# A hybrid attention block: three weight halvings moved to VectorE, two loads asked for earlier, one halving held back

## The chip, the cores and the metric

The kernel runs on one core of a Trainium2 chip. The time is that of the device for one execution, in microseconds (us). A core has five engines that run side by side and wait for each other through semaphores: TensorE (PE) multiplies matrices, VectorE (DVE), ScalarE (ACT) and GpSimd (POOL) work element by element, and SyncE (SP) only asks for transfers (DMA). Each engine takes its instructions in the order in which they stand in its queue. All DMAs of this kernel are asked for by SP, so they too have one order.

## What is computed

One decoder layer over 512 positions and 16 leading learned positions, width 1024: a projection, two attention branches with 16 heads each, a gated sum, and an output projection.

```python
u = rmsnorm(h, pre_norm_g)
cq, ckv, k_pe_raw, z_mla, fq, fk, fv, f_logit, z_fox, gate_a, gate_b = split(u @ w_in)
o_mla = causal_attention(q_m, k_m, v_mla, MLA_SCALE)          # q, k, v from cq, ckv, k_pe_raw
y_mla = (o_mla * silu(z_mla)) @ w_br_mla
cum = cumsum(log_sigmoid(f_logit + fox_forget_b))
o_fox = causal_attention(fq, fk, fv, FOX_SCALE, cum)          # logit[t,s] += cum[t] - cum[s]
y_fox = (o_fox * silu(z_fox)) @ w_br_fox
mixed = (sigmoid(gate_a) * y_mla + sigmoid(gate_b) * y_fox) @ w_out
h = h + rmsnorm(mixed, post_norm_g)
```

## The kernel before

**Precision.** Products are made from two 16-bit or 32-bit halves of each number: a high half (a rounded copy) and a low half (what the copy lost), in three matmuls: high by high, high by low, low by high. So each unit of weights, 128 columns of `w_in` (128 x 1024 numbers, 512 KB), is first loaded (`wraw`), then *halved*. For the class `Halved` this goes in steps: a bound of the numbers is found (`peak`, by ScalarE into `junk` or by VectorE's reduction at line 203), a small matmul into the `scale` bank with lines 216 to 219 makes it a power of two (`sc`), ScalarE writes the high half (line 258), and the low half follows in `lower`: on GpSimd in two instructions (lines 271 and 272, the first of which overwrites `wraw`), or on VectorE in one (line 269). Which of them it is stands in `low[0]`. While the list `deferred` is not empty, the low half isn't issued but put on that list, to be issued later. `held` names an instruction behind which a low half must stand.

**Stages.** After an opening that normalizes the input and makes the small projections, 16 stages run, one for each pair of heads and each branch, in turn FoX (`br` 1) and MLA (`br` 0): `stages`, numbered `si`. A stage has, in TensorE's order, the scores of its own pair (`st`, into six PSUM banks: two of `acc`, `b0`, `b1`, `c0`, `c1`), then the product with the values of the *stage before* (`ov`), and then a `fill`: the projections that later stages need. A FoX stage fills with the gates' projections `z` (`za`, `zb`) of this pair and `mq`, `mk`, `v` of the next MLA stage; an MLA stage fills with `fq`, `fk`, `v` of the next FoX stage. In the first stage the `fill` also has the first output gate, `pg`.

Scores go from PSUM to SBUF by VectorE (`evict`, line 979: `sf`, with the row bound `nb`), ScalarE takes exponentials (line 1014), VectorE inverts the sums (lines 1018 and 1019: `su`, `ri`), and the normalized probabilities become two 16-bit halves in `pn`: the 16 leading columns by GpSimd (`mt`, lines 1034 to 1039), the rest by ScalarE (high, line 1049) and VectorE (low, line 1053). Four DMA transposes per stage write them to `pt` (line 98); a further one writes the values' halves `vh` (lines 903 to 912, from the banks `c0` and `c1`) to `vp`. `ov` needs both, and its result is taken up by VectorE at line 1089 (`gT`). In the first stage `pt` also serves as room for the rotary product of MLA's queries, whose halves GpSimd writes to `gT` (lines 854 and 110) when `pg` has read the last of the input's 32-bit copies, whose room `gT` takes; they go through DRAM (`qpe_dram`) to `QP`.

**Order.** TensorE's instructions stand as the program issues them. On the other engines a scheduler orders them by priority: what is issued under `tc.high_priority` goes ahead, `tc.issue_after(x)` puts an instruction behind `x`. Loads stand in SP's queue where `w.load()` is called, once the transfers there are kept in program order.

**Weights ahead.** `sets[si]` are the units whose peaks are found and whose halving begins in stage `si`: for the first stage (`si` 0) the q, k and v of the third stage (`si` 2); for the second stage the two z of the second pair, which the third stage's `fill` uses. The first three loads of `sets[0]` are asked for in the opening; the two of `sets[1]` and three of `sets[2]` in the first stage, behind its four `pt` transposes. The first two units of `sets[0]` are halved at the end of the first stage's `fill` (the last two entries), the third in the second stage (`middles`). `first_z` are the two gates' weights z of the first pair. The low half of the first of them (`w_865` below) is put off and issued by VectorE at the end of the opening. Raw weights rotate through a few rooms; the fifth load counted from `sets[0]` takes the room that held the first of `first_z`.

Of the kernel before, what the change touches and what calls it, by code (L numbers as in the profile page):

```python
# [17 lines left out]
ALU = mybir.AluOpType  # L18
# [38 lines left out]
def block_kernel(ctx: ExitStack, tc: tile.TileContext, x, meta_tokens, pre_norm_g, w_in, fox_forget_b,  # L57
# [665 lines left out]
    with ExitStack() as att:  # L723
# [146 lines left out]
        def v_unit(br, pr):  # L870


            st = {}
            if br == 0:
                get = lambda: by_k(mw[pr][3], 1)
                nk, act = 1, ckv_act
            else:
                nk = KD
                get, act = (win_w(O_FV, pr), u_act) if pr else (early, both_act)

            def done(i, ps):
                if i == 0:
                    st["sc"] = aw.tile([128, 16], F32, tag="vsc", name=f"vsc{br}{pr}", bufs=4)
                    st["ps"] = ps
                sc = st["sc"]
                nc.vector.tensor_reduce(out=sc[:, i : i + 1], in_=ps, op=ALU.max, axis=AX.X, apply_absolute_value=True)
                if i == 0:
                    return
                nc.vector.tensor_scalar(out=sc[:, 2:3], in0=sc[:, 0:1], scalar1=sc[:, 1:2], scalar2=None, op0=ALU.max)
                nc.vector.tensor_single_scalar(out=sc[:, 2:3].bitcast(I32), in_=sc[:, 2:3].bitcast(I32),  # L890
                                               scalar=0x7F800000, op=ALU.bitwise_and)
                nc.vector.tensor_scalar(out=sc[:, 2:3], in0=sc[:, 2:3], scalar1=2.0 ** -100, scalar2=2.0 ** -14,
                                        op0=ALU.max, op1=ALU.mult)
                nc.vector.reciprocal(sc[:, 3:4], sc[:, 2:3])

                if br and pr:
                    nc.gpsimd.tensor_scalar(out=sc[:, 4:5], in0=sc[:, 2:3], scalar1=get.r, scalar2=2.0 / PSCALE, op0=ALU.mult,
                                            op1=ALU.mult)
                else:
                    nc.gpsimd.tensor_scalar(out=sc[:, 4:5], in0=sc[:, 2:3], scalar1=1.0 / PSCALE, scalar2=None, op0=ALU.mult)  # L900

                lead = st["ps"][:, 0:META]
                nc.scalar.activation(vh[:, 0, 0:64].rearrange("p (r c) -> p r c", c=32)[:, :, 0:META],
                                     lead.unsqueeze(1).broadcast_to([128, 2, META]), AF.Copy, scale=sc[:, 3:4])
                parts = [(vh[:, 0, 64 : 64 + META], lead, vh[:, 0, 0:META])]
                for q, p in enumerate((st["ps"][:, META:], ps)):
                    p = p.rearrange("p (j c) -> p j c", c=128)
                    hi, lo = (vh[:, 4 * q + 1 : 4 * q + 5].rearrange("p (j l) c -> p j l c", l=2)[:, :, l] for l in range(2))
                    nc.scalar.activation(hi, p, AF.Copy, scale=sc[:, 3:4])  # L909
                    parts.append((lo, p, hi))  # L910
                for lo, p, hi in parts:
                    nc.vector.scalar_tensor_tensor(out=lo, in0=p, scalar=sc[:, 3:4], in1=hi, op0=ALU.mult, op1=ALU.subtract)  # L912
                vsc[br, pr] = sc

            def tr():
                dma(vps[br], vh.rearrange("p t c -> p (t c)"), nc.sync.dma_start_transpose)
            return unit(f"v{br}{pr}", get, act, nk, ALLT, done, two("c")), [(0, tr)]
# [247 lines left out]
        def by_vector(w):  # L1165
            low[0] = nc.vector
            w()
            low[0] = nc.gpsimd

        def loads_of(ws):  # L1170
            return call(*[w.load for w in ws])
        fills, middles = [], []
        for si, (br, pr) in enumerate(stages):
            last = si + 1 == len(stages)
            ws = sets[si]
            if br == 1:
                za, zb = zs[pr]
                q, k, v = feeds[si + 1]
                fill = (vts[br, pr] if pr else begun) + za + q + zb[:3] + k + zb[3:5] + v + (call(ws[0]) if si else []) + zb[5:] + (call(ws[0]) if not si else []) + call(lambda ws=ws, p=stages[si + 1]: after_keys(ws[1], p[1]))
                middles.append([])  # L1180
            else:
                q, k, v = last_gates if last else feeds[si + 1]
                if last:
                    fill = vts[br, pr] + q + k + call(ws[0].scale, *[lambda w=w: by_vector(w) for w in ws]) + v
                else:
                    fill = vts[br, pr] + q + k[:KD] + v[:4] + call(ws[0].scale, ws[0]) + v[4:8] + call(lambda n=si + 1: peaks(sets[n][2:], nc.vector)) + v[8:] + call(ws[1]) + k[KD:]
                middles.append([sets[si - 1][2]])
            if br and si:
                fill += sum(map(loads_of, sets[si + 2 : si + 3]), [])
            if si == 5:  # L1190
                pe, rest1, store1, _ = pe_unit(1)
                fill[24:24] = pe
            fills.append(fill)
# [34 lines left out]
        deferred[:] = [None]  # L1228
        first_z[0]()
        run(opening[len(pe0) + KD : -4])  # L1230
        low[0] = nc.vector
        deferred.pop()()
        deferred.clear()
        low[0] = nc.gpsimd
        cycle[0] = 7
        loads[0] = 0
        for w in sets[0]:
            w.load()
        run(opening[-4:])
        behind.clear()  # L1240
# [1 line left out]
        for si, (br, pr) in enumerate(stages):  # L1242
# [7 lines left out]
            if si == 0:  # L1250

                run(begun)
                gT += [const.tile([128, KD, S], F32, tag=f"tokenuT{n}", name=f"gT{i}") for i, n in enumerate("hl")]
                run(fill[4:5])
                run(vts[1, 0] + pe_rest)
                between.append(lambda: load_qp(0))
                n0()
                low[0] = nc.vector
                for ahead_ in [fn.prep for _, fn in fill[5:] if hasattr(fn, "prep")][:2]:
                    first[:] = [60]  # L1260
                    with tc.issue_after(whole[0]):
                        ahead_()
                    first.clear()
                low[0] = nc.gpsimd
                n1()
                with tc.issue_after(turned_p[0]):
                    bias(1)
                peaks(sets[0], nc.scalar)
                run(fill[5:9])
                for w in sets[1] + sets[2]:  # L1270
                    w.load()
                run(fill[9:])
            else:
                run(fill[:3])
                if si == 3:
                    with tc.issue_after(turned_p[0]):
                        stores(4, 8)
                run(fill[3:5])
                if si == 1:

                    behind[:] = exps[:1]
                if si == 2:
                    behind.clear()
                n0()
                if pr and not (br or last):
                    bias(pr + 1)
                if br:
                    sets[si][0].scale()
                for job in middles[si]:
                    job()  # L1290
                if not br and si > 1:
                    run(loads_of(sets[si]))
                run(fill[5:9])
                run(fill[9:11])
                if si == 5:
                    pe[0][1].prep()
                if br:

                    behind[:] = [halved[("k", 1, pr), 1]]
                run(fill[11:12])  # L1300
                if br:
                    behind.clear()
                n1()
                if not br:
                    if last:
                        peaks(sets[si][:1], nc.scalar)
                        peaks(sets[si][1:], nc.vector)
                    else:
                        peaks(sets[si], nc.scalar)
                        peaks(sets[si + 1][:1], nc.vector)  # L1310
                        with tc.issue_after(lowered[("q", 1, pr + 1), 0]):
                            peaks(sets[si + 1][1:2], nc.vector)
                if not (br or last):
                    masked_bias()
                if 6 <= si < 8:

                    written[0] = True
                    rest1(si - 6)
                    written[0] = False
                if 8 <= si < 10:  # L1320
                    written[0] = True
                    with tc.issue_after(turned_p[0]):
                        store1(si - 8, 2, 8)
                    written[0] = False
                run(fill[12:])
# [376 lines left out]
```

## Time and profile before

| | us |
|---|---|
| median of 3 runs | 587.65 (587.45 to 588.69) |
| profiled execution | 587.34 |
| its span, first to last instruction | 585.6 |
| TensorE busy | 565.6 |
| VectorE busy | 469.1 |
| ScalarE busy | 391.0 |
| GpSimd busy | 242.9 |

The rows of the profile's views have the engine, the line of the kernel, the operation, the tile written and the tiles read (`out<-in`), the shape, and how many equal instructions are counted together (`x`). In a timeline the first two numbers are start and length in us from the start of the span, and in brackets stands how long the engine was idle before and who ended that. Line 104 is every matmul, line 98 every transfer kept in order. Busy shares are averages over stages with different limits; a gap on TensorE has to be found in its own stage.

### The profile page before, as it was taken

To read this page: it belongs to the slowest core of one execution; us is meant where nothing else is said; L and a number is where in the kernel's file an instruction comes from. 1 tells how busy PE (TensorE), PEld (TensorE's weight loads), DVE (VectorE), ACT (ScalarE), POOL (GpSimd) and SP (SyncE) were. 2 spreads that over 40 slices of the span, in tenths; PEclk is the share of its full clock that TensorE was granted. 3 is DMA by queue.
4 is the path that set the end of the run, shared out by engine and by line. 5 is a ranking of instruction groups with operands and counts; after the bars stand their busy time and mean duration, and the time that the engine had idled before them with its cause. 6 is when DMAs were issued, how large, how long until landed. Compare 5 with 4: busy or idle time off the path is not lost.

```text
span 585.6 us, 11322 instructions
## 1 busy us (share of the span) xinstructions
PE 565.6 (97%) x3864; PEld 401.6 (69%) x3864; DVE 469.1 (80%) x1248; ACT 391.0 (67%) x859; POOL 242.9 (41%) x352
## 2 busy tenths in 40 slices
PE   8999989799999999999999999999999999999995
PEld 6988556556766667658567676644776775688884
DVE  6868789669788889887797888779958987468966
ACT  7867796678787777876876878874443463343762
POOL 4422757565685697774756846800000000000000
PEclk9999998899999999999999999999999999999998
DMA  8515699969999789899998895857933230333603
GB/s 294 112 53 154 173 176 309 236 138 236 170 212 249 159 183 170 187 209 179 223 248 184 162 222 128 183 109 234 307 106 108 73 109 1 107 109 108 216 0 144
DMA packets 220026, 97.74 MB, mean 167 GB/s; under 512 B 131353, under 2 KB 209569, under 8 KB 219969
## 3 DMA queue, kind: packets, MB, share of 16 engines
q1 hardware_dynamic: 219968, 97.03, 69.5%
q8 instruction: 30, 0.49, 0.3%
q14 instruction: 28, 0.22, 0.1%
HBM read 62.62 MB, written 4.23 MB: 114 GB/s over the span
## 4 chain that ended last, share of the span: by engine, by line
PE 83%; DVE 7%; DMA 4%; issue 2%; ACT 2%; POOL 2%; SPq 0%; DVEq 0%; POOLq 0%
PE z L104 17%; PE pg L104 10%; PE v L104 7%; PE py L104 7%; PE fk L104 7%; PE fq L104 7%; PE x L104 6%; PE st L104 6%; PE ov L104 6%; DMA pt<-pn 3%; PE psm L104 2%; PE mq L104 2%; PE y L104 2%; DVE w L269 1%; PE mk L104 1%
## 5 line engine op out<-in xcount | busy, mean ns | idle before, releaser
L104 PEld LDWEIGHTS <-w 128*128 128x128 f16 x1584 | 150.1, 98 | 114.5 <-issue 4.3
L1014 ACT ACTIVATE sf<-sf,nb 128x272 f32<-128x272 f32 (+3 forms) x128 | 72.6, 569 | 21.5 <-DVE nb L979 19.2
L272 POOL TENSOR_TENSOR w<-wraw,w 128x1024 f16<-128x1024 f32 x38 | 81.5, 2144 | 2.5
L104 PE MATMUL z<-hTh,w 128*128 128x512 f16 x256 | 82.4, 382 | 0.0
L1053 DVE SCALAR_TENSOR_TENSOR pn<-sf,ri,pn 128x512 f16<-128x512 f32 (+3 forms) x128 | 74.1, 637 | 2.1 <-ACT pn L1049 2.1
L104 PE MATMUL pg<-hTh,w 128*128 128x512 f16 x240 | 72.6, 379 | 0.8 <-DVE w L269 0.8
L219 POOL TENSOR_SCALAR sc<-sc,su 128x2 f32<-128x2 f32 (+2 forms) x22 | 8.3, 378 | 142.6 <-DVE sc L216 142.4
L258 ACT ACTIVATE w<-wraw,sc 128x1024 f16<-128x1024 f32 x43 | 48.3, 1144 | 24.2 <-DVE sc L218 18.4
L1049 ACT ACTIVATE pn<-sf,ri 128x128 f16<-128x128 f32 (+3 forms) x128 | 59.7, 547 | 5.2 <-issue 3.8
L271 POOL TENSOR_SCALAR wraw<-wraw,sc 128x1024 f32<-128x1024 f32 x38 | 43.3, 1140 | 23.6 <-ACT w L258 22.4
L104 PE MATMUL z<-hTl,w 128*128 128x512 f16 x128 | 48.8, 381 | 0.0
L110 DVE TENSOR_TENSOR wl<-wraw,w 128x512 fp32r<-128x512 f32 (+1 forms) x44 | 38.5, 881 | 11.9 <-PE scale L104 4.1
L104 PE MATMUL pg<-hTl,w 128*128 128x512 f16 x120 | 45.5, 379 | 0.0
L104 PE MATMUL ov<-pt,vp 128*64 128x512 f16 (+4 forms) x416 | 35.8, 327 | 8.1 <-DMA pt<-pn 6.0
L104 PE MATMUL st<-hlk,hlq 64*128 64x272 f32 (+4 forms) x480 | 42.2, 299 | 1.1 <-DVE vh L912 1.1
L104 PE MATMUL fk<-hTh,w 128*128 128x272 f16 (+1 forms) x224 | 40.1, 276 | 0.0
L104 PE MATMUL v<-hTh,w 128*128 128x272 f16 (+1 forms) x224 | 39.3, 276 | 0.0
L104 PEld LDWEIGHTS <-vp 128*64 128x64 f16 (+1 forms) x416 | 23.9, 116 | 22.1 <-issue 13.0
L104 PEld LDWEIGHTS st<-hlk,hlq 64*128 64x128 f32 x480 | 33.5, 186 | 6.6 <-ACT vh L909 2.8
L104 PE MATMUL fq<-hTh,w 128*128 128x512 f16 x112 | 34.7, 381 | 0.0
L1405 ACT CAST w<-wraw 128x512 fp32r<-128x512 f32 x28 | 16.7, 616 | 23.5 <-DVE wraw L1414 19.0
L165 ACT CAST w<-wraw 128x1024 fp32r<-128x1024 f32 (+1 forms) x20 | 20.2, 1014 | 17.0 <-PE py L104 15.3
(342 smaller groups left out, 1476.7 us busy)
## 6 DMA issues: line engine op xcount, KB each, us to landing
wraw<-in_w_in_dram SPq DMA_DIRECT2D x47, 512.0 KB
room<-in_w_in_dram SPq DMA_DIRECT2D x9, 512.0 KB
cbp<-c_dram SPq DMA_DIRECT2D x16, 264.0 KB
wraw<-in_w_br_fox_dram SPq DMA_DIRECT2D x8, 512.0 KB
tb<-in_w_out_dram SPq DMA_DIRECT2D x8, 512.0 KB
wraw<-in_w_br_mla_dram SPq DMA_DIRECT2D x8, 512.0 KB
wraw<-in_w_out_dram SPq DMA_DIRECT2D x6, 512.0 KB
QP<-qpe_dram SPq DMA_DIRECT2D x8, 256.0 KB
```

What stands on the lines that cost most here:

```text
L104: nc.tensor.matmul(*a, **k)
L110: return eng.tensor_tensor(out=lo, in0=src, in1=f32(hi), op=ALU.subtract)
L165: nc.scalar.copy(wh[:, :n], raw[:, :n])
L219: nc.gpsimd.tensor_scalar(out=r, in0=t, scalar1=su[:, 5:6], scalar2=1.0, op0=ALU.mult, op1=ALU.mult)
L258: self.hi = nc.scalar.activation(hi, raw, AF.Copy, scale=self.s).ins
L269: nc.vector.scalar_tensor_tensor(out=lo, in0=raw, scalar=self.s, in1=hi, op0=ALU.mult, op1=ALU.subtract)
L271: nc.gpsimd.tensor_scalar(out=raw, in0=raw, scalar1=self.s, scalar2=1.0, op0=ALU.mult, op1=ALU.mult)
L272: nc.gpsimd.tensor_tensor(out=lo, in0=raw, in1=hi, op=ALU.subtract)
L1014: exps[b // 3] = nc.scalar.activation(sf, sf, AF.Exp, bias=sums["nb"][:, h, b : b + 1], scale=-1.0, accum_out=sums["su"][:, h, b : b + 1]).ins
L1049: normed[:] = [nc.scalar.activation(hi, sf, AF.Copy, scale=rib).ins]
L1053: nc.vector.scalar_tensor_tensor(out=lo, in0=sf, scalar=rib, in1=hi, op0=ALU.mult, op1=ALU.subtract)
L1405: nc.scalar.copy(to[0], src)
```

## The change

Four things are done. The low half of the first of `first_z` is now held behind the last instruction that writes `vh` in the opening (`lowered["v"]`). The loads of `sets[1]` are asked for in the opening, behind those of `sets[0]`, and only those of `sets[2]` in the first stage. The low halves of `sets[0]` (the third stage's q, k and v) are made by VectorE instead of GpSimd: the first two are put off from the first stage's end to the second stage, where they are issued right behind the scores, the third is made in the second stage as before but by VectorE. Last, in the second stage the scale and the first halving of the next z units stand behind four more steps of `v`.

```diff
@@ v_unit, done @@
                 for lo, p, hi in parts:
-                    nc.vector.scalar_tensor_tensor(out=lo, in0=p, scalar=sc[:, 3:4], in1=hi, op0=ALU.mult, op1=ALU.subtract)
+                    lowered["v"] = nc.vector.scalar_tensor_tensor(out=lo, in0=p, scalar=sc[:, 3:4], in1=hi, op0=ALU.mult, op1=ALU.subtract).ins
@@
+        def lower_by_vector():
+            low[0] = nc.vector
+            for fn in deferred[1:]:
+                fn()
+            deferred.clear()
+            low[0] = nc.gpsimd
+
@@ fills of the MLA stages @@
-                    fill = vts[br, pr] + q + k[:KD] + v[:4] + call(ws[0].scale, ws[0]) + v[4:8] + call(lambda n=si + 1: peaks(sets[n][2:], nc.vector)) + v[8:] + call(ws[1]) + k[KD:]
+                    fill = vts[br, pr] + q + k[:KD] + v[:4] + (call(ws[0].scale, ws[0]) + v[4:8] if pr else v[4:8] + call(ws[0].scale, ws[0])) + call(lambda n=si + 1: peaks(sets[n][2:], nc.vector)) + v[8:] + call(ws[1]) + k[KD:]
@@ opening @@
         run(opening[len(pe0) + KD : -4])
-        low[0] = nc.vector
-        deferred.pop()()
-        deferred.clear()
-        low[0] = nc.gpsimd
+        held[:] = [lowered["v"]]
+        lower_by_vector()
+        held.clear()
         cycle[0] = 7
         loads[0] = 0
-        for w in sets[0]:
+        for w in sets[0] + sets[1]:
             w.load()
@@ first stage @@
-                for w in sets[1] + sets[2]:
+                for w in sets[2]:
                     w.load()
-                run(fill[9:])
+                run(fill[9:-2])
+                deferred[:] = [None]
+                run(fill[-2:])
             else:
+                if si == 1:
+                    lower_by_vector()
                 run(fill[:3])
...
                 for job in middles[si]:
-                    job()
+                    by_vector(job) if si == 1 else job()
```

The instructions of TensorE are the same but for the place of one `scale` matmul; ScalarE's are the same. On the other queues the change shows at these places.

VectorE at the end of the opening, before (`v_827` and `v_867` are the two halves of the first FoX values, `vsc` their scale, `w_865` the first gate's weights):

```order
L886 TENSOR_REDUCE vsc_852<-v_827 128x1
L269 SCALAR_TENSOR_TENSOR w_865<-wraw_817,sc_819,w_865 128x1024
L886 TENSOR_REDUCE vsc_852<-v_867 128x1
L889 TENSOR_SCALAR vsc_852<-vsc_852 128x1
L890 TENSOR_SCALAR vsc_852<-vsc_852 128x1
```

And VectorE there now, down to the first score eviction:

```order
L886 TENSOR_REDUCE vsc_852<-v_827 128x1
L886 TENSOR_REDUCE vsc_852<-v_867 128x1
L889 TENSOR_SCALAR vsc_852<-vsc_852 128x1
L890 TENSOR_SCALAR vsc_852<-vsc_852 128x1
L892 TENSOR_SCALAR vsc_852<-vsc_852 128x1
L894 RECIPROCAL vsc_852<-vsc_852 128x1
L912 SCALAR_TENSOR_TENSOR vh<-v_827,vsc_852,vh 128x16
L912 SCALAR_TENSOR_TENSOR vh<-v_827,vsc_852,vh 128x2x128
L912 SCALAR_TENSOR_TENSOR vh<-v_867,vsc_852,vh 128x2x128
L269 SCALAR_TENSOR_TENSOR w_865<-wraw_817,sc_819,w_865 128x1024
L979 ISA sf_931,nb_928<-st_933,cbp_745 128x144
```

The gate's halving went from between the two reductions to between the last `vh` and the first eviction.

VectorE at the start of the second stage now (`w_1181` and `w_1183` are the third stage's q and k weights; before, line 979 followed line 912 there without a halving between them):

```order
L912 SCALAR_TENSOR_TENSOR vh<-v_1147,vsc_1145,vh 128x2x128
L269 SCALAR_TENSOR_TENSOR w_1181<-wraw_905,sc_1067,w_1181 128x1024
L269 SCALAR_TENSOR_TENSOR w_1183<-wraw_907,sc_1067,w_1183 128x1024
L979 ISA sf_1188,nb_1185<-st_1190,maskt 128x272
L979 ISA nb_1185 128x1
```

Though issued behind the scores, the two halvings stand ahead of all of that stage's evictions; the third stands ahead of its `pn`.

SP from the second stage's bias loads (`cbp`) to its first `pt` transpose, before (`wraw_1079` and `wraw_1081` are `sets[1]`, the next three `sets[2]`):

```order
L1103 DMA cbp_746<-c_dram 128x528
L98 DMA wraw_1079<-in_w_in_dram 128x8x128
L98 DMA wraw_1081<-in_w_in_dram 128x8x128
L98 DMA wraw_1083<-in_w_in_dram 128x8x128
L98 DMA wraw_1085<-in_w_in_dram 128x8x128
L98 DMA wraw_1087<-in_w_in_dram 128x8x128
L98 DMA_TRANSPOSE vp_760<-vh 128x9x128
L98 DMA wraw_1604<-in_w_uq_dram 128x2x192
L98 DMA wraw_1604<-in_w_ukv_dram 128x256
L98 DMA wraw_1763<-in_w_in_dram 128x8x128
L98 DMA QP<-qpe_dram 128x512
L98 DMA wraw_1765<-in_w_in_dram 128x8x128
```

And SP at the same place now:

```order
L1103 DMA cbp_746<-c_dram 128x528
L98 DMA wraw_1083<-in_w_in_dram 128x8x128
L98 DMA wraw_1085<-in_w_in_dram 128x8x128
L98 DMA_TRANSPOSE vp_760<-vh 128x9x128
L98 DMA wraw_1087<-in_w_in_dram 128x8x128
L98 DMA wraw_1601<-in_w_uq_dram 128x2x192
L98 DMA wraw_1601<-in_w_ukv_dram 128x256
L98 DMA wraw_1760<-in_w_in_dram 128x8x128
L98 DMA QP<-qpe_dram 128x512
L98 DMA wraw_1762<-in_w_in_dram 128x8x128
L98 DMA_TRANSPOSE pt<-pn_756 128x6x128
```

Two of the seven 512 KB loads that stood ahead of the second stage's `pt` transposes are gone from there (they stand ahead of the first stage's `vp` now, behind the first three), and `vp` went ahead of one.

## The prediction

> **What bounds the kernel now.** I read the page first.
>
> ```profile
> PE 565.6 (97%) x3864; PEld 401.6 (69%) x3864; DVE 469.1 (80%) x1248; ACT 391.0 (67%) x859; POOL 242.9 (41%) x352
> PEclk9999998899999999999999999999999999999998
> wraw<-in_w_in_dram SPq DMA_DIRECT2D x47, 512.0 KB
> ```
>
> TensorE is busy for 97% of the span, so the time can fall only where TensorE stands still or runs at a lower clock. Each digit of the clock row is 14.6 us; the two eights, 88 to 117 us, are the only dip before the end. Next, whom TensorE waits for, in the view of waits:
>
> ```profile
> PE ov L104 <- DMA pt<-pn: 6.0, 3, 4.0
> PE st L104 <- DVE vh L912: 1.1, 1, 1.1
> ```
>
> Then where these stand, in the chain of work between 55 and 135 us (start, length, what):
>
> ```profile
> 63.31 0.61 DVE vh L912 x2
> ...
> 64.06 1.11 PE st L104 x6
> ...
> 85.11 1.95 issue
> 87.05 3.46 PE ov L104 x26
> ...
> 106.66 6.19 DMA pt<-pn
> ...
> 112.99 3.84 PE ov L104 x26
> ```
>
> There are three gaps, all in the first three stages: 1.1 us before 64.06 (the first stage's third set of scores waits for VectorE to empty the value banks), 1.95 before 87.05 (the second stage runs the first stage's `ov`; its transposed probabilities `pt` land only then), and 3.97 before 112.99 (the same, one stage later). A fourth loss is the clock, in the windows (last columns: granted clock, DMA share, GB/s):
>
> ```profile
> 86.00:90.00 4.00, 2.95 (x22) 2.17 (x24) 2.31 (x9) 4.00 (x12) 3.92 (x3) 0.68 0.84 251
> 90.00:94.00 4.00, 4.00 (x24) 1.89 (x21) 3.83 (x7) 3.34 (x9) 3.93 (x10) 0.89 1.15 345
> 110.00:114.00 4.00, 1.01 (x6) 0.61 (x8) 2.90 (x21) 3.91 (x14) 2.12 (x5) 0.67 1.07 249
> 114.00:118.00 4.00, 4.00 (x27) 2.25 (x23) 1.08 (x4) 0.23 (x1) 0.16 (x1) 0.50 1.10 282
> 118.00:122.00 4.00, 4.00 (x20) 1.83 (x19) 3.14 (x9) 4.00 (x9) 2.72 (x9) 0.98 0.12 30
> ```
>
> After the gaps of 1.95 and 3.97 the clock is halved for a while; after the gap of 1.1 it is not (the clock row shows nines there).
>
> **The change, part by part.** *First gate held.* VectorE halves the first gate's weights between the two reductions of `v`; now it does so behind the last `vh`.
>
> ```profile
> 59.36 1.94 DVE L269 SCALAR_TENSOR_TENSOR w<-wraw,sc,w 128x1024 f16<-128x1024 f32 x1 [0.94 <-ACT w L258]
> 63.30 1.02 DVE L912 SCALAR_TENSOR_TENSOR vh<-v,vsc,vh 128x16 f16<-128x16 f32 x3 [0.83 <-POOL cbm L1112]
> 67.99 1.17 POOL L854 CAST gT<-pt 128x512 fp32r<-128x512 f32 x2 [3.41 <-PE pg L104]
> 74.08 4.09 SPq L98 DMA_TRANSPOSE pt<-pn  x2
> ```
>
> `vh` ends 1.94 earlier, more than the 1.1 TensorE waits, so the gap goes. Queued behind the held instruction are the score evictions; they do not get later, since as much went from in front of them. The gate's own matmuls come behind `pg`, which ends at 67.99: over 3 us to spare. Whether the end gains depends on the next gap: TensorE must not merely arrive 1.1 earlier at the same `pt`. GpSimd's casts at 67.99 wait for `pg` on TensorE and so move with it, and the transposes at 74.08 follow that GpSimd chain. So `ov` at 87.05 moves by nearly as much, and the gap of 1.95 stays. Bounds: 0 (all swallowed at 87) and 1.1. I take **1.05**, near the gap's own row, as all links follow TensorE.
>
> *Two loads a stage sooner, and the third stage's weights off GpSimd.* Both work on the 3.97:
>
> ```profile
> 58.44 4.05 SPq L98 DMA_DIRECT2D wraw<-in_w_in_dram  x3
> 85.50 7.53 SPq L98 DMA_DIRECT2D wraw<-in_w_in_dram  x5
> 99.09 10.87 SPq L98 DMA_TRANSPOSE pt<-pn  x4
> 120.44 7.85 SPq L98 DMA_TRANSPOSE pt<-pn  x4
> 84.93 2.13 POOL L272 TENSOR_TENSOR w<-wraw,w 128x1024 f16<-128x1024 f32 x1
> 98.14 0.80 POOL L1038 TENSOR_TENSOR pn<-mt,pn 128x96 f16<-128x96 f32 x1
> 106.76 2.26 PE L104 MATMUL st<-hlk,hlq 64*128 64x272 f32 x30
> ```
>
> The four transposes are asked for from 99.09 to 109.96 and have landed at 112.85 (106.66 + 6.19). Two things hold them: the SP queue, which is full from 85.5 on with five loads in front, and GpSimd's last part of `pn`, done at 98.94. Two of the five loads go: 512 KB at 345 GB/s is 1.52 each, **3.04** together. GpSimd loses three halvings (the row at 84.93 is the longer half of one), so its part is no longer last. With the 1.05 from before, `pt` lands at 112.85 - 3.04 - 1.05 = 108.76, while TensorE, now done with the scores at 106.76 + 2.26 = 109.02, arrives at 107.97: a rest of 0.8. But the four transposes took 7.85 to ask for in the next stage, with a queue less full, against 10.87 here: up to 3.0 more, and no rest. I take a rest of 0.3, so **3.67** of the 3.97. Bounds: 0 (they move only as TensorE does) and 3.97.
>
> The two loads now stand in front of the first stage's `vp` and `pt` transposes. They cost the same 3.04 there, asked for from 62.5. The three loads before them and they need 5 x 1.52 = 7.6 from 58.44, with about one load's worth of bias loads ahead, and so end near 68; the transposes are wanted from 73. That idle queue is the cover; without it the first stage's `pt` comes up to 3.04 late. The second of them also takes the room of the first gate's raw weights, and so waits for the held halving, with `vp` behind it in SP's queue; that halving is over by 64.3 as all of VectorE's work there, and `vp` is read at 87. I take 0.
>
> *Clock.* `ov` takes 3.84 after the gap; at full clock:
>
> ```profile
> 134.37 2.04 PE L104 MATMUL ov<-pt,vp 80*64 80x512 f16 x26
> ```
>
> That is 1.8 more, and z runs at half clock for another 1.4 us, losing 0.7: **2.5** that go with the gap, if the rest is short. Bounds 0 and 2.5. The half clock after 87.05 stays with its gap.
>
> *VectorE.* It takes on three halvings, two in front of the second stage's score evictions, one in front of its `pn`:
>
> ```profile
> L269 DVE SCALAR_TENSOR_TENSOR w<-room,sc,w x9: 1276/1278/1289, 419.9 to 494.4; 128x1024 f16<-128x1024 f32 x9
> 89.16 1.24 DVE L1018 SCALAR_TENSOR_TENSOR su<-su 128x6 f32<-128x6 f32 x1 [0.78 <-ACT sf L1014]
> 91.32 7.40 DVE L1053 SCALAR_TENSOR_TENSOR pn<-sf,ri,pn 128x512 f16<-128x512 f32 x8
> 138.79 4.40 DVE L1053 SCALAR_TENSOR_TENSOR pn<-sf,ri,pn 128x512 f16<-128x512 f32 x8
> 106.21 1.02 DVE L912 SCALAR_TENSOR_TENSOR vh<-v,vsc,vh 128x16 f16<-128x16 f32 x3 [0.72 <-ACT vh L909]
> ```
>
> 3 x 1.28 = 3.84 (5.82 at the 1.94 of the row at 59.36). Against that, the eight `pn` took 7.40 beside GpSimd's halvings and take 4.40 two stages later, and the small `su` took 1.24, a microsecond too much, beside one of them: 3.0 + 1.0 back. Even, so `vh` at 106.21 stays and no score waits for it. I take 0. Without that cover it is the slow rival below.
>
> *Scale moved* behind four more steps of v:
>
> ```profile
> 100.01 0.17 PE L104 MATMUL scale<-sc,spread 128*128 128x2 bf16 x1
> 101.96 0.14 DVE L216 TENSOR_SCALAR sc<-scale 128x2 int32<-128x2 int32 x1
> ```
>
> Its result lies 1.9 us unread; twelve matmuls of 0.12 are 1.4. Nothing.
>
> *What is late next.* With 7 us gone, stage three's own transposes (120.44) must follow:
>
> ```profile
> 113.29 0.61 ACT L1014 ACTIVATE sf<-sf,nb 128x400 f32<-128x400 f32 x1
> ```
>
> Its exponentials end at 113.9 whatever TensorE does; today the rest waits for `ov`. So the transposes can come 4 earlier, issued by 128.29 - 4 = 124.3, and landing some 2.9 later (as 109.96 to 112.85), at 127.2; TensorE reaches 134.37 - 7.2 = 127.2. No margin: I charge **0.2**.
>
> *Sum.* 1.05 + 3.67 + 2.5 - 0.2 = 7.0. The profiled execution took 587.34 (span 585.6), the median is 587.65: 587.34 - 7.0 = 580.3, and 0.3 for the median: **580.6**. Later gaps of `ov` (2.0 together, in the row of 6.0) move rigidly with TensorE, as their transposes wait for what TensorE produces.
>
> **Rivals.** *Partial.* The transposes get only half of the 3.97, 2.0 remain and with them the half clock, as after the gap of 1.95: 1.05 + 2.0 = 3.0 off, 584.6. For it: the DMA share is over 1 in those windows, so fewer loads may just let others fill the queue. Against: the loads removed are a large part of it. The windows show 0.68 right after a gap of 1.95, so I price a gap of 2 with the half clock. The Trainium skill, TensorE: Matmul & The Clock Gate, What's actually happening, states that the clock falls after at least one idle window of about 3.4 us. By that rule a rest of 2.0 keeps the full clock and this rival gives 584.6 - 2.5 = 582.1; the trace does not agree with it at 87.
>
> *More.* The 1.95 shrinks too, if the first stage's transposes gain more than TensorE does: up to 1.95, and 3.46 - 2.04 = 1.4 of clock: 577.2. Little speaks for it, since the GpSimd chain follows TensorE.
>
> *Nothing.* The first gap is swallowed at 87 and the second stays, because the transposes, not the loads, fill the queue: 587.6. Against: GpSimd's 98.94 and five loads stand plainly in front of 99.09.
>
> *Slower.* VectorE becomes the bound in the second stage: each halving takes 1.94, nothing comes back, and `vh` at 107.23 ends 5.8 later, at 113.0. The next scores wait for it as those at 64.06 did, `ov` starts at 114.1 instead of 112.99 with the half clock kept: 588.8. It decides from 4.7 late on. Against: the halvings leave GpSimd, and the 1.94 was measured beside GpSimd's work of 58.9 to 62.6. The Trainium skill, SBUF — State Buffer, SBUF: two separate sides, states that a VectorE instruction with two SBUF inputs and a GpSimd instruction that reads SBUF lock each other out whole. By that rule each halving can lose one of the GpSimd instructions that remain, 0.80 as at 98.14: 3 x 2.08 = 6.2 in place of 5.8, and 589.2; that the eight `pn` took 7.40 against 4.40 agrees with a lock.
>
> **How the numbers follow.** Forecast 0.58 (own range 579.0 to 582.5), partial 0.17, more 0.08, nothing 0.09, slower 0.08. The range reaches from the fast rival to the partial one, 577.0 to 585.0, and leaves out 0.17. A measurement of this kernel tells about 0.2% from no change: faster 0.83, same 0.09, slower 0.08.
>
> **What would show it.** First step: no wait of `st` for `vh`, and `ov` near 86.0. Second: five loads in the SP queue near 58 and two near 84.5, `pt` transposes asked for by 96, `ov` of the third stage near 108 with under 1 us of waiting. Clock: 1.00 from 94 on. VectorE: eight `pn` in under 5 us although a halving stands ahead. Wrong would be a first-stage `pt` that is no earlier (1.95 grows to 3), a wait of `st` for `vh` near 107, or a new wait of `ov` near 127.

## The result, and the profile after

| | before | after |
|---|---|---|
| median, us | 587.65 | 580.46 (580.19 to 582.48) |
| profiled execution, us | 587.34 | 580.54 |
| its span, us | 585.6 | 578.8 |
| mean granted clock | 0.989 | 0.995 |

The ratio of the times is 0.988, with a 95% interval from 0.985 to 0.991: the changed kernel is 7.2 us faster, against 7.0 forecast. A fourth run of the kernel before took 640.87 us, far above the others, and is left out as a slow one. The clock row of the changed kernel has one eight where two stood side by side:

```profile
PE 563.0 (97%) x3864; PEld 399.8 (69%) x3864; DVE 468.0 (81%) x1251; ACT 390.8 (68%) x859; POOL 232.1 (40%) x346
PEclk9999998999999999999999999999999999999999
```

Whom TensorE waits for, in the view of waits (total, times, longest):

```profile
PE ov L104 <- DMA pt<-pn: 4.7, 4, 2.4
PE scale L104 <- DVE hlk L110: 0.6, 1, 0.6
```

The wait of `st` for `vh` is gone, and the longest wait of `ov` is now that of the first stage. The second row is new, and the prediction did not name it: at 80.05 TensorE waits for VectorE's `hlk`. Every profile with the gate held has this wait of 0.6 to 0.7 in the `scale` matmul, and none without has it. Then SP's queue in the timeline (start, length, what):

```profile
56.92 0.80 SPq L1103 DMA_DIRECT2D cbp<-c_dram  x2
58.17 7.03 SPq L98 DMA_DIRECT2D wraw<-in_w_in_dram  x5
...
72.34 4.32 SPq L98 DMA_TRANSPOSE pt<-pn  x2
...
77.61 5.96 SPq L98 DMA_TRANSPOSE pt<-pn  x2
...
85.07 1.04 SPq L98 DMA_DIRECT2D wraw<-in_w_in_dram  x2
...
94.20 11.42 SPq L98 DMA_TRANSPOSE pt<-pn  x4
```

Five loads stand near 58 and two near 85, as the change says. The third stage's four transposes, the row at 94.20, are asked for earlier than at 99.09, and take 11.42 to ask for where they took 10.87. And the chain of work through the first three stages:

```profile
80.21 6.31 DMA pt<-pn
86.66 2.66 PE ov L104 x26
...
108.62 1.97 PE ov L104 x26
110.59 2.70 PE z L104 x12
113.29 2.61 PE z L104 x12
...
127.50 1.97 PE ov L104 x26
```

No transfer stands ahead of the third stage's `ov` at 108.62 any more, and it runs at full clock. To compare executions, times are counted below from SP's ask for the first bias loads, the row `cbp` at 56.92 here. In the kernel before that row is:

```profile
57.19 0.81 SPq L1103 DMA_DIRECT2D cbp<-c_dram  x2
```

The steps of its chain that were not shown ahead are:

```profile
116.83 3.39 PE z L104 x12
...
120.22 2.61 PE z L104 x12
...
134.44 1.97 PE ov L104 x26
```

So counted, the first stage's `ov` went from 29.86 to 29.74, the third stage's from 55.80 to 51.70, and the second group of z behind it (120.22 before, 113.29 now) from 63.03 to 56.37. The gain is therefore 0.12 up to the first `ov`, 3.98 more up to the third, and 2.56 in that `ov` (3.84 to 1.97) and the z behind it (3.39 to 2.70). From there everything moves along: the fourth stage's `ov` starts 6.67 earlier, the span is 6.8 shorter.

### The profile page after: what moved, and what is told of

It is laid out like the page before. It is cut to its first block, busy times and chain, and to the rows that moved or that the text cites. A ratio compares the mean times of both kernels' runs of the same rounds, so it can differ in the third digit from the quotient of the medians.

```text
span 578.8 us, 11317 instructions
## 1 busy us (share of the span) xinstructions
PE 563.0 (97%) x3864; PEld 399.8 (69%) x3864; DVE 468.0 (81%) x1251; ACT 390.8 (68%) x859; POOL 232.1 (40%) x346
## 4 chain that ended last, share of the span: by engine, by line
PE 77%; DVE 8%; DMA 5%; ACT 4%; issue 2%; POOL 2%; SPq 1%; DVEq 0%; ACTq 0%; POOLq 0%
PE z L104 15%; PE pg L104 10%; PE py L104 8%; PE fq L104 7%; PE v L104 7%; PE x L104 6%; PE fk L104 6%; PE st L104 5%; PE ov L104 5%; DMA pt<-pn 4%; PE psm L104 2%; PE mq L104 2%; PE y L104 2%; DVE w L269 1%; DVE wl L110 1%
## 5 line engine op out<-in xcount | busy, mean ns | idle before, releaser
L272 POOL TENSOR_TENSOR w<-wraw,w 128x1024 f16<-128x1024 f32 x35 | 74.9, 2141 | 2.3
L1053 DVE SCALAR_TENSOR_TENSOR pn<-sf,ri,pn 128x512 f16<-128x512 f32 (+3 forms) x128 | 70.9, 611 | 1.6 <-ACT pn L1049 1.6
L271 POOL TENSOR_SCALAR wraw<-wraw,sc 128x1024 f32<-128x1024 f32 x35 | 39.8, 1136 | 20.5 <-ACT w L258 19.4
L104 PE MATMUL ov<-pt,vp 128*64 128x512 f16 (+4 forms) x416 | 33.2, 311 | 4.7 <-DMA pt<-pn 4.7
L104 PEld LDWEIGHTS <-vp 128*64 128x64 f16 (+1 forms) x416 | 22.3, 111 | 17.7 <-issue 6.9
```

The costliest lines, as they stand in the source:

```text
L104: nc.tensor.matmul(*a, **k)
L271: nc.gpsimd.tensor_scalar(out=raw, in0=raw, scalar1=self.s, scalar2=1.0, op0=ALU.mult, op1=ALU.mult)
L272: nc.gpsimd.tensor_tensor(out=lo, in0=raw, in1=hi, op=ALU.subtract)
L1053: nc.vector.scalar_tensor_tensor(out=lo, in0=sf, scalar=rib, in1=hi, op0=ALU.mult, op1=ALU.subtract)
```

## The experiments

Three groups of four kernels ran, each group on one chip beside its own runs of the kernel before, so totals are given as ratios to that, with their 95% intervals. The times of the kernel before spread over 4.5 to 7.5 us within a group, so the reading goes by the profiles, one for each kernel: when an `ov` starts after the ask for the bias loads, and how long TensorE stood idle before it. The changed kernel was not run on the first group's chip; that group's totals can only be set beside its ratios on two others, 0.988 and 0.986.

### One part of the change undone

**The gate.** The halving goes back between the two reductions:

```diff
-        held[:] = [lowered["v"]]
-        lower_by_vector()
-        held.clear()
+        low[0] = nc.vector
+        deferred.pop()()
+        deferred.clear()
+        low[0] = nc.gpsimd
```

> The changed kernel with the first gate's halving back between the two reductions of v. Theory S (swallowed: the first stage's transposes land at their own time, near 86.5, whatever TensorE does before): the wait of st for vh of 1.1 us is back at 64, the gap before the first stage's ov shrinks from 2.4 to between 1.3 and 1.9, that ov starts at 86.6 +- 0.3, total as the changed kernel, 580.5 +- 0.5. Theory P (the prediction's own step): ov starts 1.05 later, at 87.7, total 581.5. Rival R: the halving that runs earlier frees its room earlier for the fifth load, so the first stage's vp and pt come earlier, ov at 86.2 or less, total 579.5 to 580.3.

Ratio 0.992 (0.989 to 0.995). From the timeline (in brackets how long TensorE was idle, and who ended it):

```profile
57.64 0.80 SPq L1103 DMA_DIRECT2D cbp<-c_dram  x2
...
64.52 1.11 PE L104 MATMUL st<-hlk,hlq 64*128 64x400 f32 x6 [1.20 <-DVE vh L912]
...
87.90 3.44 PE L104 MATMUL ov<-pt,vp 80*64 80x512 f16 x26 [1.93 <-DMA pt<-pn]
```

The wait for `vh` is back, and `ov` starts 30.26 after the ask, 0.52 later than the 29.74 of the changed kernel. That lies between S (no change) and P (1.05 later); R falls. The total, 3.5 us under the kernel before, is worse than P's 581.5, but its interval overlaps that of the changed kernel.

**The loads.** Both go back behind the first stage's transposes:

```diff
-        for w in sets[0] + sets[1]:
+        for w in sets[0]:
...
-                for w in sets[2]:
+                for w in sets[1] + sets[2]:
```

> The changed kernel with the two loads of sets[1] back in the second stage's queue. Theory Q (additive: the loads carry 3.04 of the 3.97, GpSimd's part the rest): the third stage's ov has a gap of about 3.0 again and the half clock with it, total 580.5 + 3.0 + 2.5 = 586.0. Theory B (both ends in one: the transposes wait for whichever of queue and GpSimd is later): gap 3.5 to 4, total 586.5 to 587.3. Rival G (GpSimd's part alone carried it): gap under 1, total 581 or less. For the first stage, theory L (the two early loads slow its transposes): ov of the first stage starts 0.5 to 1.0 earlier than the changed kernel's 86.66, at 85.7 to 86.2; theory S (they have a landing time of their own): no change.

Ratio 0.999 (0.997 to 1.001): without the loads the rest of the change is worth nothing that can be measured. From the timeline:

```profile
57.48 0.80 SPq L1103 DMA_DIRECT2D cbp<-c_dram  x2
...
86.14 2.04 PE L104 MATMUL ov<-pt,vp 80*64 80x512 f16 x26 [1.79 <-issue]
...
111.34 3.84 PE L104 MATMUL ov<-pt,vp 80*64 80x512 f16 x26 [4.45 <-DMA pt<-pn]
```

The gap before the third stage's `ov` is whole again, 4.45, so G falls, Q's 3.0 is too little, and B's 3.5 to 4 is the nearest. The first `ov` starts at 28.66, 1.08 earlier than in the changed kernel. The size is a little above L's 0.5 to 1.0; S falls.

**VectorE's halvings** go back to GpSimd: the three low halves are no longer put off, and `middles` are issued as before.

```diff
-                run(fill[9:-2])
-                deferred[:] = [None]
-                run(fill[-2:])
+                run(fill[9:])
             else:
-                if si == 1:
-                    lower_by_vector()
                 run(fill[:3])
...
-                    by_vector(job) if si == 1 else job()
+                    job()
```

> The changed kernel with the three low halves of sets[0] back on GpSimd. Theory Q (additive): GpSimd's pn part ends at 98.7, transposes asked for from there in a queue that is less full, gap before the third stage's ov about 1, without much half clock: 581.5 to 582.5. Theory B (both ends in one): the transposes are asked for no earlier than before, gap 3 to 4 and the half clock with it: 585.5 to 587. In both the eight pn of VectorE take over 6 us again.

Ratio 0.991 (0.988 to 0.993). The third stage's `ov` waits for nothing, although VectorE's `pn` is as slow as before the change:

```profile
87.39 1.24 DVE L1018 SCALAR_TENSOR_TENSOR su<-su 128x6 f32<-128x6 f32 x1 [0.79 <-ACT sf L1014]
90.26 7.16 DVE L1053 SCALAR_TENSOR_TENSOR pn<-sf,ri,pn 128x512 f16<-128x512 f32 x8
...
107.68 2.04 PE L104 MATMUL ov<-pt,vp 80*64 80x512 f16 x26
```

Both Q (a gap of 1) and B (3 to 4) are wrong: with the loads out of the way, GpSimd's part of `pn` leaves no gap. (Q's total, 581.5 to 582.5, is met with 582.20, but not for Q's reason.) GpSimd still sets the ask: SP waits 0.9 for its part of `pn`, which ends at 96.36, and at 96.36 the transposes are asked for, 39.64 after the bias loads, where the changed kernel has 37.28. They land in time all the same.

**The scale** goes four steps of v earlier again (the expression for the MLA stages' `fill` as before the change).

> The changed kernel with the scale and the first z halving four steps of v earlier, as before the change. Theory: nothing, 580.5 +- 0.4, the scale matmul near 99.7 with no wait. Rival: TensorE, some 5 us earlier now, waits there for the bounds that ScalarE finds (ended at 97.4), or the halving comes in front of VectorE's other work and vh of the third stage is late: 0.5 to 1.3 us more, 581 to 581.8.

Ratio 0.990 (0.988 to 0.993); the `scale` matmul stands at 97.92, with no wait. The third stage's `ov` waits 0.24 for its transposes. No cost of the old place is seen in the trace.

### One part of the change alone

These are the kernel before with one part of the diff: the gate; the loads; the halvings on VectorE with the scale. The fourth is the changed kernel once more.

> The kernel before with the first gate's halving held behind vh, and nothing else. Counted from the ask for the first bias loads (57.19 in before, 56.92 in after) the first stage's ov started at 29.86 before, at 29.74 with the whole change, and at 28.66 where the loads were put back. Theory L (the held halving does bring the ov earlier by its 1.05, and the two early loads take that back): ov at 28.7 +- 0.3, the third stage's ov keeps a gap of 3.5 to 4.5, total 0.5 to 1.5 us under before. Theory S (the transposes land at their own time): ov at 29.9 +- 0.3, total as before.

Ratio 0.997 (0.994 to 0.999), 2 us. From the timeline:

```profile
57.04 0.80 SPq L1103 DMA_DIRECT2D cbp<-c_dram  x2
...
72.44 3.70 SPq L98 DMA_TRANSPOSE pt<-pn  x2
...
77.09 5.65 SPq L98 DMA_TRANSPOSE pt<-pn  x2
...
85.83 3.71 PE L104 MATMUL ov<-pt,vp 80*64 80x512 f16 x26 [1.90 <-issue]
```

`ov` starts 28.79 after the ask, 1.07 earlier than in the kernel before, and the gap of 1.9 stays. That is L, and it is the prediction's own step. That it meets 1.05 within 0.02 us is luck: two profiles with gate and loads as before differ by 0.34. The third stage's gap is 3.34, a little under L's 3.5 to 4.5.

> The kernel before with the two loads of sets[1] asked for in the opening, and nothing else. Theory L: the first stage's ov 0.4 to 0.8 later than the 29.86 of before, at 30.2 to 30.7; the third stage's ov with a gap under 0.5 and its own half clock gone; total 4.5 to 6 us under before on the same chip. Theory Q (loads and GpSimd's part add up): a gap of about 1 stays there, total 3 to 4.5 under before. If the loads cost the first stage nothing, its ov stays at 29.9.

Ratio 0.989 (0.986 to 0.993): three quarters of the change come from this part. From the timeline:

```profile
56.86 0.80 SPq L1103 DMA_DIRECT2D cbp<-c_dram  x2
...
87.07 3.11 PE L104 MATMUL ov<-pt,vp 80*64 80x512 f16 x26 [2.36 <-DMA pt<-pn]
...
97.81 0.80 POOL L1038 TENSOR_TENSOR pn<-mt,pn 128x96 f16<-128x96 f32 x1
98.64 8.50 SPq L98 DMA_TRANSPOSE pt<-pn  x4
...
109.25 2.04 PE L104 MATMUL ov<-pt,vp 80*64 80x512 f16 x26 [0.20 <-DMA pt<-pn]
```

The third stage's gap is 0.20 where it was 3.97, and Q's gap of 1 does not show. The first `ov` starts at 30.21, 0.35 later than in the kernel before; L says 30.2 to 30.7, but so small a step is within the spread of profiles. The transposes were asked for 41.78 after the bias loads, about as in the kernel before (99.09 - 57.19 = 41.90). So here they land sooner with less in the queue ahead of them, and not by being asked for sooner. What holds the ask now is GpSimd: its last part of `pn` ends at 98.61, and SP waits 1.3 for it, after 2.5 for one of GpSimd's halvings, whose room a load in between takes.

> The kernel before with the three low halves of sets[0] on VectorE and the scale moved, without the loads and the gate. Theory L (the queue alone sets the third stage's transposes): GpSimd's pn part ends some 5 us earlier, the transposes are asked for when the five loads are through, as before, gap 3.5 to 4.5, total within 0.7 of before. Theory Q: gap about 3, total 0.9 to 1.5 under before. Slower rival: VectorE's work late, vh of the third stage late, 0.5 or more above before.

Ratio 0.999 (0.996 to 1.001). From the timeline:

```profile
56.77 0.80 SPq L1103 DMA_DIRECT2D cbp<-c_dram  x2
...
86.97 2.04 PE L104 MATMUL ov<-pt,vp 80*64 80x512 f16 x26 [2.00 <-issue]
...
93.69 4.05 DVE L1053 SCALAR_TENSOR_TENSOR pn<-sf,ri,pn 128x128 f16<-128x128 f32 x8
...
98.88 10.49 SPq L98 DMA_TRANSPOSE pt<-pn  x4
...
112.26 3.84 PE L104 MATMUL ov<-pt,vp 80*64 80x512 f16 x26 [4.78 <-DMA pt<-pn]
```

`pn` is 3.4 shorter, GpSimd's last part of it ends at 95.06, and the transposes are still asked for at 42.11, behind the queue, and awaited for 4.78 (L: 3.5 to 4.5). L's mechanism holds: here the queue alone decides. With the loads moved it is GpSimd that sets the ask, so there were two bounds on it, side by side. Where both are lifted and the gate is as before (the first kernel of the first group), the transposes are asked for at 96.42, 38.78 after the bias loads. The third `ov` starts at 55.49, and at 52.39 with the loads alone: the two loads are worth 3.1 more than the halvings there.

> The changed kernel as it is, once more, for a second profile and for times on the same chip as the parts. Ov of the first stage at 29.5 +- 0.4 after the ask for the bias loads, no gap before the third stage's ov, total 5.5 to 7 under before. Whether the clock is halved behind the first stage's gap of some 2 us may differ between executions: so far it was after gaps of 1.95, 2.42, 1.93 and 2.17, and was not after 2.12 and 1.79; a halved window of 3.4 us costs some 1.7.

Ratio 0.986 (0.983 to 0.989), median 580.37. By the ratio the gain is about 8 us, more than the 5.5 to 7 expected. The first `ov` starts 29.35 after the ask, behind a gap of 2.33; the third has none.

### The first stage's gap filled

If the gap before the first `ov` is nothing but waiting, TensorE can do other work there. In the first of these kernels (fill_first) it runs the first steps of the second stage's `fill` ahead of that `ov`.

```diff
             sc()
-            for fn in late:
-                fn()
+            if si not in (1,):
+                for fn in late:
+                    fn()
...
                 run(fill[3:5])
+                if si in (1,):
+                    for fn in late:
+                        fn()
```

The second (fill_two) has `(1, 2)` there, the third (fill_all) `range(1, 15)`. The fourth (loads_fill) has the latter in the kernel before, with the early loads alone.

> The changed kernel with the first stage's ov moved in TensorE's order behind the first four steps of the second stage's fill (12 matmuls of fq, 2.6 us). Theory L (the first stage's gap is pure waiting for the transposes, and the halved clock behind it comes from the gap): the gap of 2.1 to 2.4 is under 0.5, no half clock near 88, and TensorE comes some 2.2 to 4 earlier to the third stage's ov, whose transposes come at their own time (near 50.2 after the ask for the bias loads): a gap of 1.5 to 2.9 appears there. Total 0 to 2 under the changed kernel. Rival: the fq steps wait themselves (their halvings on VectorE, or a bank that the evictions still read), total as the changed kernel or worse.

Ratio 0.989 (0.985 to 0.993). The first gap is gone (`ov` at 87.1 directly behind `fq`, granted clock 1.00 from 82 to 106), and 0.92 is waited before the third `ov`, less than L's 1.5 to 2.9. But nothing is gained in total, as the rival said, though `fq` waits for nothing; the next one shows why.

> As fill_first, and the second stage's ov behind the first four steps of the third stage's fill (12 matmuls of z, 2.6 us). Theory L: both gaps under 0.7, no half clock up to 130, total 2.2 to 4.5 under the changed kernel (ratio to before 0.977 to 0.984). Rival: the gap appears one stage later still, at the fourth stage's ov, total under 2 gained.

Ratio 0.988 (0.984 to 0.992). The timeline of TensorE, and of ScalarE behind it:

```profile
97.32 0.16 PE L104 MATMUL scale<-sc,spread 128*128 128x2 bf16 x1 [0.60 <-ACT junk L201]
105.29 0.53 PE L104 MATMUL st<-hlk,hlq 64*128 64x288 f32 x4 [1.35 <-ACT hlk L385]
...
101.18 2.19 ACT L258 ACTIVATE w<-wraw,sc 128x1024 f16<-128x1024 f32 x2 [3.54 <-DVE sc L218]
...
104.06 0.82 ACT L909 ACTIVATE vh<-v,vsc 128x256 f16<-128x256 f32 x2
104.77 0.47 ACT L385 ACTIVATE hlk<-fk,sc 128x256 fp32r<-128x256 f32 x1
```

Both gaps before `ov` are covered. TensorE comes to the `scale` matmul 4.3 us earlier (39.75 after the ask for the bias loads, 44.08 in the changed kernel), and now waits 0.60 for ScalarE's bounds and 1.35 for its `hlk`, which stands on ScalarE behind two halvings and the values' `vh`. Neither theory had that wait, and the half clock comes back behind it (0.57 granted from 106 to 110). L's total (0.977 to 0.984) is missed; the rival's, under 2 us gained, holds, but no gap stands at the fourth stage's `ov`.

> As fill_two, in every stage but the last. Theory L: the remaining waits of ov for pt (2.3 in three later stages of the changed kernel) go too, total 0 to 2.5 under fill_two. Rival: the later ov keeps the room of pt busy longer, so that the next transposes come late: total over fill_two.

Ratio 0.987 (0.984 to 0.991). The same waits stand at 97 and 105. Of the later waits of `ov` for `pt` 0.6 is left, but the total can't be told from that of fill_two or of the changed kernel.

> The kernel before with the two loads asked for early and ov moved as in fill_all, without the held gate, without VectorE's halvings and without the moved scale. Theory L: the gate's 1.15 at 64 is no longer swallowed by a gap at the first ov, so without the gate this is 0.8 to 1.5 over fill_all, with a wait of st for vh of 1.1; VectorE's halvings and the scale change nothing. If the halvings do matter: 1 us more on top, or a wait of TensorE for w or pn that fill_all does not show.

Ratio 0.989 (0.986 to 0.993). TensorE's waits:

```profile
PE v L104 <- POOL w L272: 1.6, 1, 1.6
PE fq L104 <- POOL w L272: 1.4, 1, 1.4
PE st L104 <- DVE vh L912: 1.2, 1, 1.2
```

With the gap filled, TensorE meets GpSimd's halvings (1.4 and 1.6), which VectorE does in time in fill_all. So TensorE does wait for the halvings once it is that early; before, the gap hid them. The wait for `vh` shows as expected. The total is 1.3 us above that of fill_all, within the intervals. No version tried here was faster than the changed kernel.

## Why the prediction came out right

*Two loads a stage sooner, and the weights off GpSimd: 3.67 of 3.97.* The gap went whole. The two loads do it nearly alone, and the prediction's price for them, 3.04, is near what they measured (3.1 against the halvings alone, 3.4 against the kernel before, whose third `ov` started at 55.80). Taking the halvings off GpSimd was not needed for the gap: alone it brings nothing, and without it no gap comes back. Of the rest of 0.8 that the prediction left after the loads, the kernel with the loads alone shows 0.20: its transposes landed 3.4 earlier, and TensorE arrived 0.36 later (51.83 before, 52.19 with the loads, each the start of `ov` less its gap).

That two things held the ask, the queue and GpSimd's part of `pn`, was read rightly. With the gate as before, the transposes are asked for 41.90 after the bias loads with neither lifted, at 41.78 with the loads alone, at 42.11 with the halvings alone, and at 38.78 with both. With the gate held too, in the changed kernel, it is 37.28: 4.62 earlier in all, where the prediction had 3.04 + 1.05 = 4.09. Its last term failed, the shorter ask in a less full queue (7.85 in place of 10.87): the four transposes take 8.50 with the loads alone, but 11.42 in the changed kernel, which so loses 0.55 of the 4.62 again. Why they take longer there was not tried.

*Clock: 2.5.* Measured 1.87 and 0.69, so 2.56. It went with the gap. The half clock behind the first gap stayed, as forecast.

*First gate held: 1.05.* This step failed in the changed kernel, where `ov` came 0.12 earlier (0.51 in its second profile) and the gap grew from 1.95 to 2.42, on the way to the 3 that was to show the step wrong. Its mechanism was right: alone it moved `ov` by 1.07 with the gap kept. The term that was wrong is the one next to it, the two loads in front of the first stage's transposes, taken at 0. The four cases, with every profile of the kernels of the first two groups (start of the first `ov` after the ask for the bias loads):

| | gate as before | gate held |
|---|---|---|
| loads as before | 29.86, 30.20 | 28.79, 28.66 |
| loads early | 30.21, 30.26 | 29.74, 29.03, 29.60, 29.35 |

The early loads cost 0.7 with the gate held (means 28.73 and 29.43) and 0.2 without. Within one cell the profiles differ by up to 0.7, so these sizes are rough; that no profile with the early loads is as early as the two without, where the gate is held, is plain. The cover named for them, an SP queue free again near 68, was there for the ask of these transposes: the transposes are asked for 15.42 after the bias loads in the changed kernel and 15.40 with the gate alone. But the two pairs then take 4.32 and 5.96 to ask for, in place of 3.70 and 5.65. Whether the loads' own bytes or the stores of `gT`, pushed later by them, slow the transposes wasn't tried.

*VectorE: 0.* Even, as forecast. Three halvings came (2.48 and 1.65), and `pn` and `su` gave back:

```profile
82.11 2.48 DVE L269 SCALAR_TENSOR_TENSOR w<-wraw,sc,w 128x1024 f16<-128x1024 f32 x2
89.92 0.19 DVE L1018 SCALAR_TENSOR_TENSOR su<-su 128x6 f32<-128x6 f32 x1 [0.86 <-ACT sf L1014]
90.96 1.65 DVE L269 SCALAR_TENSOR_TENSOR w<-wraw,sc,w 128x1024 f16<-128x1024 f32 x1
92.54 4.05 DVE L1053 SCALAR_TENSOR_TENSOR pn<-sf,ri,pn 128x128 f16<-128x128 f32 x8
105.82 1.02 DVE L912 SCALAR_TENSOR_TENSOR vh<-v,vsc,vh 128x16 f16<-128x16 f32 x3 [0.72 <-ACT vh L909]
```

`pn` took 7.40 and takes 4.05, `su` 1.24 and now 0.19, and `vh` stands at 105.82 (106.21 before). With the halvings back on GpSimd both are slow again (7.16 and 1.24). The trace agrees with the rule of the Trainium skill, SBUF — State Buffer, SBUF: two separate sides, that a VectorE instruction with two SBUF inputs and a GpSimd instruction that reads SBUF lock each other out. The price that the prediction worked out by that rule for the slow rival, 2.08 for each halving, did not come: they took 1.24 to 1.65.

*Scale moved: 0.* No effect was seen. *What is late next: -0.2.* No wait came at the fourth stage's `ov`.

So the sum came out by errors of opposite sign: 0.93 too much for the first gap, since the loads' cost there was left out, against 0.3 kept in the second gap and 0.2 charged behind it that did not come. In the two profiles this makes 6.7, not 7.0. The 7.2 between the medians has an interval of 5.2 to 8.8, so that near a hit is in part luck. Of the rivals, *partial* falls with the third stage's gap, which left nothing, *more* with the first stage's gap, which grew, *nothing* with the loads alone, and *slower* with `vh`, which is not late.

## What to carry to other kernels

Ask what a transfer waits behind, and not only when it is asked for: with the early loads alone the four transposes were asked for at the same time as before, and landed 3 us sooner, with two loads fewer ahead of them. Where two things hold an ask side by side, moving one shows nothing at the ask until the other goes too. A load moved to a time when the queue looks free can still cost the transfers that follow (here 0.2 to 0.7 for two, where their bytes were priced at 3.04); don't put it at nothing. And a gap that is filled shows the next engine that was hidden behind it, here ScalarE with a wait of 1.35, so filling it is worth only the distance to that one.

## What the runs showed of the hardware

In these traces the granted clock changes in steps of 3.41 us, and a step in which TensorE is idle for part of the time can be enough to halve the next one. In the kernel before it changes at 87.48, 90.89, 111.37 and 118.20, which are 1, 6 and 2 such steps apart. In the windows view of the kernel before, with edges on the grid of its changes (length, busy time of TensorE, of PEld, DVE, ACT and POOL, granted clock, DMA share, GB/s):

```profile
84.07:87.48 3.41, 1.46 (x16) 1.00 (x15) 2.99 (x16) 3.41 (x12) 3.33 (x3) 1.00 0.92 176
87.48:90.89 3.41, 3.41 (x26) 2.31 (x23) 1.98 (x4) 3.29 (x8) 3.26 (x5) 0.50 0.84 266
```

And in the changed kernel with the loads put back, with the edges of its own grid, laid back from its next change at 109.79:

```profile
82.48:85.90 3.42, 1.87 (x25) 1.53 (x22) 3.35 (x8) 1.55 (x3) 0.00 (x0) 1.00 0.71 185
85.90:89.31 3.41, 3.17 (x32) 2.13 (x33) 2.99 (x17) 3.34 (x13) 0.00 (x0) 1.00 0.82 240
```

TensorE stood idle for 1.95 and 1.79 before `ov`. The first gap lies in one window, the second is cut by an edge, and only the first halves the clock. In seven profiles of ten of the kernels with a first gap of 1.8 to 2.4 the clock fell behind it, each time after a window with 1.05 to 1.51 of work. Two of the other three kept the full clock after windows with 1.87, 2.28 and 2.55, the gap being cut by an edge; the third kept it after a window with 1.44, but its grid is laid back from a change 488 us later.

How much work keeps the clock up is not settled by this. Where the first gap was filled, the clock fell in the third stage after windows with 1.63 (fill_first) and 1.88 (fill_two and fill_all), and 1.88 is no less than the 1.87 that kept it. A halved window costs some 1.7 us, half of 3.41, by estimate. That one and the same kernel gains or loses this by where the grid falls would be a part of the spread of single executions, but isn't shown: both profiles of the changed kernel lost it. The Trainium skill, TensorE: Matmul & The Clock Gate, What's actually happening, has the free-running window of 3413 ns, and the trace agrees with its length; that a whole window must be idle does not hold here.
